# A decoder layer on one core: FFN matmuls with tokens on partitions, and the attention gate's columns moved to the beginning

## The chip, the cores and the metric

One Trainium2 chip, one NeuronCore of it. The metric is the device time of one execution in microseconds (us). TensorE (PE in the rows; PEld is its weight load), VectorE (DVE), ScalarE (ACT), GpSimd (POOL) and SyncE (SP, which starts nearly all DMAs) each run their own instruction stream in order and wait for one another on semaphores.

## The reference, cut to what matters

```python
h = rms_norm(x, norm_mix_pre)                       # x: 256 tokens x 1024
proj = h @ w_in                                     # 1024 x 9232
qa, ka, va, qd, kd, vd, zd, bd, ad, ga, gd = split(proj)   # 7 x 1024, then 8, 8, 1024, 1024
ya = attention(rope(qa), rope(ka), va)              # 8 heads x 128; one causal block of 256
yd = gated_deltanet(qd, kd, vd, zd, bd, ad, ...)    # conv, chunks of 64, a recurrence
merged = sigmoid(ga) * (ya @ w_o_attn) + sigmoid(gd) * (yd @ w_o_delta)
x = x + rms_norm(merged @ w_out, norm_mix_post)
h = rms_norm(x, norm_ffn_pre)
f = (silu(h @ w_gate) * (h @ w_up)) @ w_down        # 1024 -> 2816 -> 1024
x = x + rms_norm(f, norm_ffn_post)
```

## The kernel before, in words

Every weight comes from memory once, as a list `P` of pieces of about 512 KB. `load_to` issues their DMAs on SP into four buffers (`wr`); `split_to` cuts each piece into a high and a low part, ACT writing `wh` and DVE the remainder `wl`, and `piece(j)` asks for the split of piece j + 3. Each product of an activation and a weight is then three TensorE matmuls (high by high, high by low, low by high). There are two orientations. `natural` keeps the activation stationary and streams 512 weight columns, so tokens land on partitions: 12 matmuls of 512 columns for one piece. `chan` keeps the weight stationary and streams the 256 tokens, so channels land on partitions: 24 matmuls of 256 columns for one piece.

The program runs in this order. `start` loads x and its norm weights, transposes x through TensorE into `hT` (`x_transpose`, `x_evac`), and computes the first gate block ("g", 0): 414 columns, of which the first 16 are b and a and the rest belong to the attention gate. Then come the units of `make_units`: twelve "c" units (DeltaNet's q, k, v, in `chan` form), one attention or z unit after every second of them, then the last attention value unit ("a", 1, "v"), the last z unit ("z", 1), the gate blocks 1 and 2, the two halves of `w_o_attn` ("oa"), the gate blocks 3 and 4, and the two halves of `w_o_delta` ("od"). After that `main` does `w_out`, the FFN's gate and up products, and `w_down` (`two_tile`).

The recurrent and attention work (`dn_tile`, `dn_out`, `attn`) runs beside these as side generators. `Flow` keeps a planned time while the program is written, and `pump` writes a side step as soon as its inputs are planned to be ready; so the places of side steps between the main matmuls come out of that plan and are fixed in the program. The unit ("oa", 0) begins with `yield joined(("at", 0), ("at", 1))`: as long as both attention generators have not been written out, no main matmul is written. "od" waits in the same way for the DeltaNet outputs. `start` is written under `manual_schedule`, in its exact order.

In the FFN before, the first 512 channels of gate and up are done in token form: `silu` of the gate (scaled by `rs2`, one factor for each token) and the product with up, both per token tile, then eight 128x128 transposes back (`fn`, into `fT`). The other 2304 channels are done by `chan`, block by block: 24 matmuls for a gate block and 24 for an up block into one bank, a product with the row `rsb` that `spread` prepared, `silu`, a product, and a split into `fT`.

Of the kernel before, what the change touches and what calls it, by code (L numbers as in the profile page):

```python
# [18 lines left out]
D = 1024  # L19
# [6 lines left out]
NFB = DFF // 128  # L26
PSUM = bass.MemoryType.PSUM
# [37 lines left out]
def make_units():  # L65
    dn = [("c", g, p, hp) for g in range(2) for p in "qkv" for hp in range(2)]
    at = [("a", 0, p) for p in "qkv"] + [("z", 0)] + [("a", 1, p) for p in "qkv"] + [("z", 1)]
    at += [("g", n) for n in (1, 2)]
    out = [("g", 0)]
    i = 0  # L70
    for j, d in enumerate(dn):
        out.append(d)
        if j % 2 == 1:
            out.append(at[i])
            i += 1
    out += at[i:]
    out += [("oa", 0), ("oa", 1), ("g", 3), ("g", 4), ("od", 0), ("od", 1)]
    return out
# [173 lines left out]
def build(nc, tc, ctx, A):  # L252
# [79 lines left out]
    col0 = cst.tile([128, 8], F32, name="col0")  # L332
    triur = cst.tile([128, 128], F32R, name="triur")
# [35 lines left out]
    GB = []  # L369
    c = BA  # L370
    for i, n in enumerate((414, 414, 412, 412, 412)):
        GB.append((c, n))
        c += n
# [3 lines left out]
    for u in UNITS:  # L377
        if u[0] == "g":
            natblk(u, wind, *GB[u[1]])
# [15 lines left out]
    natblk(("fn", 0), A["w_gate"][0], 0)  # L395
    natblk(("fn", 1), A["w_up"][0], 0)
# [12 lines left out]
    def load_to(i):  # L409
        while nl[0] <= min(i, len(P) - 1):  # L410
# [3 lines left out]
            SP.dma_start(t, ap)  # L414
# [17 lines left out]
    def split_halves(j):  # L432
# [5 lines left out]
        for i in range(a):  # L438
            ACT.activation(hi[:, i], r[:, i], AF.Copy)
            DVE.tensor_tensor(lo[:, i], r[:, i], hi[:, i].bitcast(F32), op=ALU.subtract)  # L440
# [8 lines left out]

    xt = []  # L450
    for t in range(2):
        xx = s4.get([128, 1024], F32, f"x{t}")
        if t == 0:
            for q in range(2):
                SP.dma_start(xx[:, 512 * q:512 * q + 512], xd[0:128, 512 * q:512 * q + 512])
                if q == 0:
                    SP.dma_start(rows0, A["norm_mix_pre"].rearrange("o (k p) -> (o k) p", p=128))
            load_to(1)
        else:
            SP.dma_start(xx, xd[128:256, :])  # L460
        xt.append(xx)
    load_to(RAW - 1)
    SP.dma_start(rows[0:96], A["conv_w"][0].rearrange("i (b p) -> (i b) p", p=128))
# [37 lines left out]
    def x_evac(bs, cols, t, his, los, q):  # L501
# [6 lines left out]
        main_put(bs[1])  # L508

# [47 lines left out]
    def natural(j0, act, outs, first=0, end=4):  # L557
        his, los = act
        for i in range(first, end):
            hi, lo = piece(j0 + i)  # L560
            for kk in range(2):
# [419 lines left out]
    def gate_evac(i, outs):  # L981
        c0, n = GB[i]
        for st, base in ((sg, GA), (sd, GD)):
            lo, hi = max(c0, base), min(c0 + n, base + D)
            if hi <= lo:
                continue
            for t in range(2):
                if t not in st:
                    st[t] = yield from slot(s4, [128, 1024], F32, f"gt{base}{t}")
                ACT.activation(st[t][:, lo - base:hi - base], outs[t][:, lo - c0:hi - c0], AF.Sigmoid, scale=rs[t])  # L990
        for t in range(2):
            main_put(outs[t])
# [58 lines left out]
    def unit_g(u):  # L1051
        outs = yield from two_banks()
        yield from natural(plan[u], hT, outs)
        yield from gate_evac(u[1], outs)
# [43 lines left out]
    def start():  # L1098
        hT.extend((yield from act_slots("h")))
        with tc.manual_schedule():  # L1100
# [14 lines left out]
            ev = []  # L1115
            for q in range(2):
                ev.append((yield from x_transpose(xt[0], q)))
            fill(FILL)
            main_put(wb)
            outs = yield from two_banks()  # L1120
            x_evac(ev[0], col0, 0, hT[0], hT[1], 0)
            pc = [split_halves(0)]
            x_evac(ev[1], col0, 0, hT[0], hT[1], 1)
            pc.append(split_halves(1))

            def part(i, t):
                hi, lo = pc[i]
                n = hi.shape[2]
                ts = slice(128 * t, 128 * t + 128)
                for kk in range(2):  # L1130
                    k = 2 * i + kk
                    ah, al = hT[0][k // 4][:, k % 4, ts], hT[1][k // 4][:, k % 4, ts]
                    mm(outs[t][:, :n], ah, hi[:, kk, :], k == 0, False)
                    mm(outs[t][:, :n], al, hi[:, kk, :], False, False)
                    mm(outs[t][:, :n], ah, lo[:, kk, :], False, k == 7)

            part(0, 0)
            e0 = yield from x_transpose(xt[1], 0)
            part(1, 0)
            e1 = yield from x_transpose(xt[1], 1)  # L1140
            x_evac(e0, col0, 1, hT[0], hT[1], 0)
            pc.append(piece(2, 0))
            x_evac(e1, col0, 1, hT[0], hT[1], 1)
            part(0, 1)
            part(1, 1)
            nrs = {}
            for i in range(2):
                pc.append(piece(3, 0)) if i == 0 else None
                part(2 + i, 0)
                part(2 + i, 1)  # L1150
            for t in range(2):
# [6 lines left out]
                split_to(4 + t)  # L1158
            ACT.activation(ex, abc, AF.Exp)
            b = yield from main_bank()  # L1160
            tr(b[:, 0:105], rows[0:105, :], ident[0:105, 0:105])
            DVE.tensor_copy(colp[:, 0:105], b[:, 0:105])
            main_put(b)
            held.append(DVE.tensor_copy(id16, ident).ins)
        s4.put(xt[0], xt[1])
        for t in range(2):
            ACT.activation(beta[:, 8 * t:8 * t + 8], outs[t][:, 0:8], AF.Exp, scale=nrs[t])
# [193 lines left out]
```

## Time and profile before

| what | us |
|---|---|
| median of 3 runs | 551.74 |
| lowest and highest | 551.53, 552.23 |
| span of the profiled execution, first to last instruction | 550.8 |
| first gate matmul begins | 9.10 |
| first "c" matmul begins (the gate block of the beginning is done) | 21.12 |
| last z unit ends, gate block 1 begins | 233.99 |
| "od" begins | 308.54 |
| FFN blocks in `chan` form | 380.43 to 484.85 |
| last matmul begins | 544.7 |

The median is 0.98 us above the span, which begins at the first instruction and ends at the last. A row of the profile gives an engine, a line of the kernel (nearly all work passes through the helper lines 131, 289 and 293, so tiles tell more than lines), the operation, output and inputs, and the shape. For a matmul the input named first streams and the second is stationary. The busy time of a matmul row includes its drain, so successive rows overlap: what a matmul costs is the distance from its start to the next start.

### The profile page before, as it was taken

To read this page: it belongs to the slowest core of one execution; us is meant where nothing else is said; L and a number is where in the kernel's file an instruction comes from. 1 tells how busy PE (TensorE), PEld (TensorE's weight loads), DVE (VectorE), ACT (ScalarE), POOL (GpSimd) and SP (SyncE) were. 2 spreads that over 40 slices of the span, in tenths; PEclk is the share of its full clock that TensorE was granted. 3 is DMA by queue.
4 is the path that set the end of the run, shared out by engine and by line. 5 is a ranking of instruction groups with operands and counts; after the bars stand their busy time and mean duration, and the time that the engine had idled before them with its cause. 6 is when DMAs were issued, how large, how long until landed. Compare 5 with 4: busy or idle time off the path is not lost.

```text
span 550.8 us, 9219 instructions
## 1 busy us (share of the span) xinstructions
PE 538.2 (98%) x3554; PEld 480.8 (87%) x3554; DVE 383.4 (70%) x687; ACT 316.1 (57%) x569; POOL 26.5 (5%) x38
## 2 busy tenths in 40 slices
PE   7999999899999999999999999999999999999995
PEld 5988898898989888899889888778999999988884
DVE  4798886896879787866576566686666666754434
ACT  5968658588654966786526444584444444443331
POOL 0001002200000230000000000010000000000000
PEclk9999999999999999999999999999999999999999
DMA  7957765245465252245466765268666666655512
GB/s 243 240 154 226 227 192 153 78 116 157 126 178 155 79 166 63 62 147 156 128 202 192 246 221 175 74 175 252 186 191 186 175 181 187 192 190 190 193 39 76
DMA packets 89598, 90.45 MB, mean 164 GB/s; under 512 B 3169, under 2 KB 69842, under 8 KB 89554
## 3 DMA queue, kind: packets, MB, share of 16 engines
q1 hardware_dynamic: 89554, 89.86, 54.7%
q8 instruction: 28, 0.46, 0.4%
q14 instruction: 16, 0.13, 0.1%
HBM read 88.80 MB, written 1.05 MB: 163 GB/s over the span
## 4 chain that ended last, share of the span: by engine, by line
PE 85%; DVE 4%; ACT 3%; DMA 3%; issue 2%; POOL 2%; SPq 0%; POOLq 0%; DVEq 0%; ACTq 0%
PE b_m L289 74%; PE b_s L289 8%; PE b_s L293 2%; DMA q_x<-in_x 1%; DVE wl L131 1%; POOL tiny L131 1%; PE b_m L293 1%; DMA K<-in_shape_k 1%; DMA wr<-in_w_in 1%; ACT wh L131 1%; ACT L131 0%; DVE h_a L131 0%; DVE q_vT L131 0%; SPq L131 0%; ACT d_js L131 0%
## 5 line engine op out<-in xcount | busy, mean ns | idle before, releaser
L131 DVE TENSOR_TENSOR wl<-wr,wh 128x1024 fp32r<-128x1024 f32 (+3 forms) x168 | 197.9, 1184 | 91.5 <-ACT wh L131 87.5
L131 ACT ACTIVATE wh<-wr 128x1024 fp32r<-128x1024 f32 (+3 forms) x168 | 171.5, 1029 | 135.0 <-PE b_m L289 92.0
L289 PE MATMUL b_m<-wh,q_hh 128*128 128x512 f32 (+2 forms) x208 | 83.3, 400 | 1.3 <-ACT wh L131 1.3
L289 PE MATMUL b_m<-q_fh,wh 128*128 128x256 f32 x288 | 81.6, 283 | 0.0
L289 PE MATMUL b_m<-q_fl,wh 128*128 128x256 f32 x288 | 81.6, 283 | 0.0
L289 PE MATMUL b_m<-q_fh,wl 128*128 128x256 f32 x288 | 81.5, 283 | 0.0
L289 PE MATMUL b_m<-wl,q_hh 128*128 128x512 f32 (+2 forms) x208 | 78.9, 379 | 0.0
L289 PE MATMUL b_m<-wh,q_hl 128*128 128x512 f32 (+2 forms) x208 | 78.9, 379 | 0.0
L289 PE MATMUL b_m<-q_hh,wh 128*128 128x256 f32 x192 | 56.3, 293 | 0.0
L289 PEld LDWEIGHTS b_m<-q_fl,wh 128*128 128x128 f32 x288 | 55.3, 192 | 0.0
L289 PEld LDWEIGHTS b_m<-q_fh,wl 128*128 128x128 f32 x288 | 55.3, 192 | 0.0
L289 PEld LDWEIGHTS b_m<-q_fh,wh 128*128 128x128 f32 x288 | 55.3, 192 | 0.0
L289 PE MATMUL b_m<-q_hl,wh 128*128 128x256 f32 x192 | 54.4, 283 | 0.0
L289 PE MATMUL b_m<-q_hh,wl 128*128 128x256 f32 x192 | 54.3, 283 | 0.0
L289 PE MATMUL b_m<-wh,q_fh 128*128 128x512 f32 x120 | 46.9, 391 | 0.5 <-DVE q_fl L131 0.5
L289 PE MATMUL b_m<-wl,q_fh 128*128 128x512 f32 x120 | 46.9, 391 | 0.0
L289 PE MATMUL b_m<-wh,q_fl 128*128 128x512 f32 x120 | 46.6, 389 | 0.0
L289 PEld LDWEIGHTS b_m<-wh,q_hh 128*128 128x128 f32 x208 | 39.7, 191 | 6.1 <-ACT wh L131 2.2
L289 PEld LDWEIGHTS b_m<-wh,q_hl 128*128 128x128 f32 x208 | 39.6, 190 | 5.3
L289 PEld LDWEIGHTS b_m<-wl,q_hh 128*128 128x128 f32 x208 | 39.7, 191 | 3.9
L131 POOL TENSOR_TENSOR tiny<-tiny,mhalf 128x4 f32<-128x4 f32 (+1 forms) x20 | 17.4, 874 | 474.6 <-DVE tiny L131 474.6
L289 PEld LDWEIGHTS b_m<-q_hh,wh 128*128 128x128 f32 x192 | 36.7, 191 | 0.4
(215 smaller groups left out, 884.3 us busy)
## 6 DMA issues: line engine op xcount, KB each, us to landing
wr<-in_w_in SPq DMA_DIRECT2D x56, 512.0 KB, 4.1
wr<-in_w_gate SPq DMA_DIRECT2D x22, 512.0 KB, 3.9
wr<-in_w_up SPq DMA_DIRECT2D x22, 512.0 KB, 3.9
wr<-in_w_down SPq DMA_DIRECT2D x22, 512.0 KB, 3.3
wr<-in_w_in SPq DMA_DIRECT2D x12, 412.0 KB, 3.4
wr<-in_w_o_attn SPq DMA_DIRECT2D x8, 512.0 KB, 4.7
wr<-in_w_o_delta SPq DMA_DIRECT2D x8, 512.0 KB, 4.4
wr<-in_w_out SPq DMA_DIRECT2D x8, 512.0 KB, 3.6
```

The costliest lines, as they stand in the source:

```text
L131: r = f(*args, **kw)
L289: issue(lambda: PE.matmul(out, l, r, start=start, stop=stop))
L293: issue(lambda: PE.transpose(out, in_, idn))
```

## The change

1. FFN: all 2816 channels of gate and up are done in token form. Five rounds of 512 channels (`NFR`), each a `natural` pass over four gate pieces and four up pieces, then one pass whose pieces hold 256 gate columns beside 256 up columns. The result of each round is transposed back by `turn`, a generator that is put in `late` and is run after the first piece of the pass that follows. The `chan` blocks, `spread` of `rs2` and the tiles `js` are gone.
2. Beginning: `start` computes all 1024 columns of the attention gate for both token tiles, in eight pieces of 128 x 1024, into four banks, with the transposes of x put between them in pairs. x and the pieces are loaded whole, alternating; the norm weights come by a DMA of the ACT queue.
3. The 16 columns b and a are loaded apart (`wba`), cut into a high and a low part in a stationary tile of 128 columns (`wbr`), and multiplied with `hT` by 16 matmuls of 256 columns; two small matmuls with `sel` bring the result to tokens on partitions.
4. Units: the gate blocks 1 to 4 are gone from between the others. "g" is now the DeltaNet gate alone, two blocks of 512 columns, behind "oa". So ("z", 1) is followed at once by ("oa", 0).

```diff
@@ make_units
-    at += [("g", n) for n in (1, 2)]
-    out = [("g", 0)]
+    out = []
...
-    out += [("oa", 0), ("oa", 1), ("g", 3), ("g", 4), ("od", 0), ("od", 1)]
+    out += [("oa", 0), ("oa", 1), ("g", 0), ("g", 1), ("od", 0), ("od", 1)]
@@ plan
+    for k in range(8):
+        plan["ga", k] = len(P)
+        P.append((wind[k * 128:(k + 1) * 128, GA:GA + D].rearrange("(k p) n -> p k n", p=128), 1, D))
...
-    for b in range(4, NFB):
-        mark(("fg", b), chn, A["w_gate"][0], b * 128)
-        mark(("fu", b), chn, A["w_up"][0], b * 128)
+    for r in range(NFR):
+        natblk(("fg", r), wg, 512 * r)
+        natblk(("fu", r), wu, 512 * r)
@@ start
+            def part(pc, t, k):
+                hi, lo = pc
+                ts = slice(128 * t, 128 * t + 128)
+                ah, al = hT[0][k // 4][:, k % 4, ts], hT[1][k // 4][:, k % 4, ts]
+                for n in range(2):
+                    sl = slice(512 * n, 512 * n + 512)
+                    mm(outs[t][n], ah, hi[:, 0, sl], k == 0, False)
+                    mm(outs[t][n], al, hi[:, 0, sl], False, False)
+                    mm(outs[t][n], ah, lo[:, 0, sl], False, k == 7)
...
+            for k in range(8):
+                for i in range(2):
+                    mm(b[:, 0:256], wbr[:, k, :], hT[i][k // 4][:, k % 4, :], k == 0 and i == 0, k == 7 and i == 1)
...
+        for t in range(2):
+            mm(b[:, 16 * t:16 * t + 16], ba[:, 128 * t:128 * t + 128], sel, True, True)
@@ main, FFN
+        def turn(r, fn, nb):
+            yield from f_slots(r)
+            for t in range(2):
+                b = yield from main_bank()
+                for i in range(nb):
+                    tr(b[:, 128 * i:128 * i + 128], fn[t][:, 128 * i:128 * i + 128], ident)
+                ts = slice(128 * t, 128 * t + 128)
+                split_out(v4(b)[:, 0:nb], fT[r][0][:, 0:nb, ts], fT[r][1][:, 0:nb, ts])
...
-        yield from spread([rs2[0], rs2[1]], rsb)
+        late.append(turn(0, fn, 4))
+        for r in range(1, NFR):
+            fn = {}
+            for w in range(2):
+                outs = yield from two_banks()
+                yield from natural(plan["fu" if w else "fg", r], h2, outs, late=late)
```

How the instructions move is seen at three places. First the SP queue at the very beginning (`q0_x0`, `q1_x1` are the two token tiles of x, `wr0` to `wr3` the first pieces), before:

```order
L131 DMA q0_x0_98<-in_x 128x512
L131 DMA rows0_77<-in_norm_mix_pre 8x128
L131 DMA q0_x0_98<-in_x 128x512
L131 DMA wr0_102<-in_w_in 128x2x414
L131 DMA wr1_104<-in_w_in 128x2x414
L131 DMA q1_x1_106<-in_x 128x1024
L131 DMA wr2_108<-in_w_in 128x2x414
```

The same place in the changed kernel:

```order
L131 DMA q0_x0_100<-in_x 128x1024
L131 DMA wr0_102<-in_w_in 128x1024
L131 DMA q1_x1_104<-in_x 128x1024
L131 DMA wr1_106<-in_w_in 128x1024
L131 DMA wr2_108<-in_w_in 128x1024
L131 DMA wr3_110<-in_w_in 128x1024
L131 DMA wba_112<-in_w_in 128x8x16
```

The first weight piece is now second in the queue instead of fourth, and pieces are 512 KB instead of 414 KB.

Second the ACT engine around the end of the last z unit. `p0` and `p1` are the attention probabilities of head group 1 (the exponentials of the first and the second token tile), `sz01` and `sz11` the two halves of the z unit's `silu`, `ydh0` an output of DeltaNet group 0, `U` and `T` tiles of the triangular inverse of group 1. Before:

```order
L131 ACTIVATE d8_p0_2767,tiny_96<-b4_s_2769,tiny_96 128x128 x4
L131 ACTIVATE scr_97,tiny_96<-d1_oA_2356 128x128 x4
L131 ACTIVATE q15_p1_2768,tiny_96<-b1_s_2818,tiny_96 128x256 x2
L131 ACTIVATE q15_p1_2768,tiny_96<-b7_s_2835,tiny_96 128x256 x2
L131 ACTIVATE wh63_2910<-wr63_2594 128x828
L131 ACT_TABLE_LOAD
L131 ACTIVATE d13_sz01_2904<-b3_m_2588,tiny_96 128x512
L131 ACTIVATE q11_ydh0_2320<-b0_s_2876,colp_95 128x4x128
```

In the changed kernel:

```order
L131 ACTIVATE scr_98,tiny_97<-d1_oA_2461 128x128 x4
L131 ACTIVATE q16_p1_2843,tiny_97<-b4_s_2923,tiny_97 128x256 x2
L131 ACTIVATE wh67_3117<-wr67_2699 128x1024
L131 ACT_TABLE_LOAD
L131 ACTIVATE d13_sz01_2984<-b5_m_2693,tiny_97 128x512
L131 ACT_TABLE_LOAD
L131 ACTIVATE q16_p1_2843,tiny_97<-b1_s_2946,tiny_97 128x256 x2
L131 ACT_TABLE_LOAD
L131 ACTIVATE d7_sz11_2986<-b2_m_2694,tiny_97 128x512
L131 ACTIVATE q12_ydh0_2425<-b0_s_2988,colp_96 128x4x128
```

The second pair of p1 exponentials now stands behind `sz01`, the first half of z, and between two more table loads. On PE, 80 side matmuls (from the transposes of `d1_oA` and one level of the inverse, over the transposes of p0 and p1 and the products with v, to the last level) stand in one run between the last z matmul and the first "oa" matmul; before, they stand among 48 gate matmuls.

Third PE at the end of the FFN's first 512 channels (`d_fn` is the token-form product, `d_dg,ones` the matmul of `spread`), before:

```order
L289 MATMUL b_m<-wh_4156,q_fh_3839 128x512
L289 MATMUL b_m<-wl_4157,q_fh_3839 128x512
L289 MATMUL b_m<-wh_4156,q_fl_3840 128x512
L289 MATMUL b_m<-d_dg,ones 128x256
L293 MATMUL b_m<-ident,d_fn_4114 128x128 x4
L289 MATMUL b_m<-q_fh_3837,wh_4180 128x256
L289 MATMUL b_m<-q_fl_3838,wh_4180 128x256
L289 MATMUL b_m<-q_fh_3837,wl_4181 128x256
```

In the changed kernel, one piece later:

```order
L289 MATMUL b_m<-wh_4129,q_fh_3788 128x512
L289 MATMUL b_m<-wl_4130,q_fh_3788 128x512
L289 MATMUL b_m<-wh_4129,q_fl_3789 128x512
L293 MATMUL b_m<-ident,d_fn_4063 128x128 x4
L293 MATMUL b_m<-ident,d_fn_4090 128x128 x4
L289 MATMUL b_m<-wh_4170,q_fh_3788 128x512
L289 MATMUL b_m<-wl_4171,q_fh_3788 128x512
L289 MATMUL b_m<-wh_4170,q_fl_3789 128x512
```

The transposes stand 12 matmuls behind the last up matmul, and matmuls of 512 columns follow; such a place comes once in every round.

## Rows read from the trace of the kernel before

**Rows 1.** The page, part 1: busy us (share of the span) and instructions.

```profile
PE 538.2 (98%) x3554; PEld 480.8 (87%) x3554; DVE 383.4 (70%) x687; ACT 316.1 (57%) x569; POOL 26.5 (5%) x38
```

**Rows 2.** Timeline of PE (start us, us, instruction): FFN in `chan` form, then `w_down`.

```profile
384.05 0.28 PE L289 MATMUL b_m<-q_fh,wh 128*128 128x256 f32 x1
...
484.85 0.40 PE L289 MATMUL b_m<-wh,q_fh 128*128 128x512 f32 x1
...
533.84 0.39 PE L289 MATMUL b_m<-wh,q_fh 128*128 128x512 f32 x1
```

**Rows 3.** Timeline of PE: gate block 4, its last three pieces, to "od".

```profile
301.76 0.34 PE L289 MATMUL b_m<-wh,q_hh 128*128 128x412 f32 x1
...
308.54 0.39 PE L289 MATMUL b_m<-wh,q_ydh 128*128 128x512 f32 x1
```

**Rows 4.** Timeline of PE: eight transposes between 512-column matmuls, in "od".

```profile
321.24 1.09 PE L293 MATMUL b_m<-ident,q_gt 128*128 128x128 f32 x8
...
322.40 0.39 PE L289 MATMUL b_m<-wh,q_ydh 128*128 128x512 f32 x1
```

**Rows 5.** Timeline of PE: `spread` and the first four `fn` transposes in the FFN.

```profile
379.65 0.59 PE L289 MATMUL b_m<-d_dg,ones 128*128 128x256 f32 x2
...
380.43 0.36 PE L289 MATMUL b_m<-q_fh,wh 128*128 128x256 f32 x1
```

**Rows 6.** Timeline of all engines: the beginning (in brackets idle before, and what ended it).

```profile
5.44 1.11 PE L293 MATMUL b_m<-ident,q_x 128*128 128x128 f32 x4 [0.56 <-DMA q_x<-in_x]
...
6.34 1.49 PE L1110 MATMUL b_m<-warm 128*128 128x512 f16 x3
...
9.10 0.71 PE L289 MATMUL b_m<-wh,q_hh 128*128 128x414 f32 x1 [1.27 <-ACT wh L131]
...
9.61 0.55 PE L289 MATMUL b_m<-wh,q_hl 128*128 128x414 f32 x1
...
9.95 0.55 PE L289 MATMUL b_m<-wl,q_hh 128*128 128x414 f32 x1
...
21.12 0.36 PE L289 MATMUL b_m<-q_hh,wh 128*128 128x256 f32 x1
```

**Rows 7.** Windows: length, busy us (count) by engine, granted clock, DMA, GB/s; the end.

```profile
544.90:549.20 4.30, 0.00 (x0) 0.00 (x0) 2.17 (x4) 0.69 (x2) 0.55 (x1) 1.00 0.27 100
549.30:550.70 1.40, 0.00 (x0) 0.00 (x0) 0.00 (x0) 0.00 (x0) 0.00 (x0) 0.50 0.11 41
```

**Rows 8.** Timeline of ACT: around the end of the last z unit.

```profile
231.08 0.48 ACT L131 ACTIVATE q_p<-b_s,tiny 128x256 f32<-128x256 f32 x1 [0.29 <-DVE tiny L131]
...
232.90 1.28 ACT L131 ACT_TABLE_LOAD   x1
234.19 0.69 ACT L131 ACTIVATE d_sz<-b_m,tiny 128x512 f32<-128x512 f32 x1
234.78 0.69 ACT L131 ACTIVATE q_ydh<-b_s,colp 128x512 fp32r<-128x512 f32 x1
235.35 0.39 ACT L131 ACTIVATE h_U<-b_s 128x256 f16<-128x256 f32 x1
...
236.14 0.72 ACT L131 ACTIVATE d_sz<-b_m,tiny 128x512 f32<-128x512 f32 x1
...
238.54 1.13 ACT L131 ACTIVATE q_pT<-b_s 128x512 f32<-128x512 f32 x2
```

**Rows 9.** Timeline of PE: last z matmuls, products with v, gate block 2's first.

```profile
232.20 0.39 PE L289 MATMUL b_m<-wh,q_hl 128*128 128x512 f32 x1
...
233.99 0.35 PE L289 MATMUL b_m<-wh,q_hh 128*128 128x414 f32 x1
...
242.43 0.68 PE L289 MATMUL b_s<-q_pT,q_av 128*128 128x256 f32 x2
...
243.74 0.44 PE L289 MATMUL b_m<-wh,q_hh 128*128 128x414 f32 x1
...
248.61 0.35 PE L289 MATMUL b_m<-wh,q_hh 128*128 128x412 f32 x1
```

More of the change, by code (lines that the diff above doesn't have):

```diff
@@ L560, in natural @@
             hi, lo = piece(j0 + i)
+            if late and i == first + 1:
+                yield from late.popleft()
             for kk in range(2):
@@ L979, in two_banks, with gate_evac @@
         return [b0, b1]
[L981 to L990, printed above, removed]
+    def gate_evac(st, n, outs):
         for t in range(2):
+            if t not in st:
+                st[t] = yield from slot(s4, [128, 1024], F32, f"gt{t}")
+            ACT.activation(st[t][:, 512 * n:512 * n + 512], outs[t], AF.Sigmoid, scale=rs[t])
             main_put(outs[t])
@@ new lines, in start @@
+            part(pc[1], 1, 1)
+            xb[0, 6] = yield from x_tr(0, 6)
+            pc.append(piece(2, 0))
+            evac(0, 4)
+            part(pc[2], 0, 2)
+            part(pc[2], 1, 2)
+            xb[1, 4] = yield from x_tr(1, 4)
+            xb[1, 6] = yield from x_tr(1, 6)
+            pc.append(piece(3, 0))
+            evac(1, 4)
+            part(pc[3], 0, 3)
+            evac(0, 6)
+            part(pc[3], 1, 3)
+            evac(1, 6)
+            pc.append(piece(4, 0))
+            part(pc[4], 0, 4)
@@ L1146, in start @@
+            part(pc[4], 1, 4)
             nrs = {}
[L1147 to L1150, printed above, removed]
             for t in range(2):
@@ L1157, in start @@
                 DVE.tensor_scalar(nrs[t], rs[t], -1.0, None, op0=ALU.mult)
-                split_to(4 + t)
+                pc.append(piece(5 + t, 0))
+                part(pc[5 + t], 0, 5 + t)
+                part(pc[5 + t], 1, 5 + t)
+            wbr = yield from slot(s4, [128, 8, 128], F32R, "wbr")
+            DVE.memset(wbr.bitcast(F32), 0.0)
+            ACT.activation(wbr[:, :, 0:16], wba, AF.Copy)
+            DVE.tensor_tensor(wbr[:, :, 32:48], wba, wbr[:, :, 0:16].bitcast(F32), op=ALU.subtract)
+            DVE.tensor_tensor(sel, ident[0:48, 0:16], ident[0:48, 32:48], op=ALU.add)
             ACT.activation(ex, abc, AF.Exp)
+            pc.append(piece(7, 1))
+            part(pc[7], 0, 7)
+            part(pc[7], 1, 7)
             b = yield from main_bank()
@@ L1163, in start @@
             main_put(b)
+            b = yield from main_bank()
+            for k in range(8):
+                for i in range(2):
+                    mm(b[:, 0:256], wbr[:, k, :], hT[i][k // 4][:, k % 4, :], k == 0 and i == 0, k == 7 and i == 1)
+            s4.put(wbr)
+            ba = yield from slot(s1, [48, 256], F32, "ba")
+            ACT.activation(ba, b[0:48, 0:256], AF.Copy)
+            main_put(b)
             held.append(DVE.tensor_copy(id16, ident).ins)
@@ L1204, in two_tile @@
                 hi, lo = piece(plan[name, k])
+                if late and k == 1:
+                    yield from late.popleft()
                 for t in range(2):
@@ L1303, in main @@
-        for b_ in range(4, NFB):
-            if b_ % 4 == 0:
-                yield from f_slots(b_)
-            b = yield from main_bank()
-            yield from chan(plan["fg", b_], h2, b[:, 0:256])
-            yield from chan(plan["fu", b_], h2, b[:, 256:512])
-            js = yield from slot(s2, [128, 2, 256], F32, "js")
-            DVE.tensor_tensor(js, b.rearrange("p (a c) -> p a c", a=2), rsb[:, None, :].to_broadcast([128, 2, 256]),
-                              op=ALU.mult)
-            main_put(b)
-            ACT.activation(js[:, 0], js[:, 0], AF.Silu)
-            DVE.tensor_tensor(js[:, 1], js[:, 1], js[:, 0], op=ALU.mult)
-            split_out(js[:, 1], fT[-1][0][:, b_ % 4, :], fT[-1][1][:, b_ % 4, :])
-            s2.put(js)
+        late.append(turn(0, fn, 4))
@@ new lines, in main @@
+        for r in range(1, NFR):
[3 more added lines that the diff above has]
+                yield from natural(plan["fu" if w else "fg", r], h2, outs, late=late)
+                for t in range(2):
+                    if w == 0:
+                        yield from gate_out(fn, t, outs[t], 512)
+                    else:
+                        up_out(fn, t, outs[t])
+                    main_put(outs[t])
+            late.append(turn(r, fn, 4))
@@ L1322, in last @@
             yield 0
-        yield from two_tile("dn", ([a for a, _ in fT], [a for _, a in fT]), NFB, 4, finish_rms(wfo, x1, last))
+        yield from two_tile("dn", lambda k, ts: [a[:, k % 4, ts] for a in fT[k // 4]], NFB, 4, finish_rms(wfo, x1, last), late)
     def later(ns, gen):
```

152 lines of the change are left out of this document (86 added, 66 removed).

## The prediction

> **What bounds the kernel now.** I read the page's busy times first: TensorE is busy for 98% of the span, the next engine for 70% [rows 1]. So the first question for each edit is how much TensorE time it adds or takes, and the second is whether an edit makes TensorE wait where it does not wait now. For the first question busy means are of no use, because a matmul's row contains its drain; I took distances between starts from the timeline. In the FFN's `chan` form 840 matmuls of 256 columns lie between 384.05 and 484.85, which is 0.120 us each; in `w_down` 216 matmuls of 512 columns lie between 484.85 and 533.84, 0.227 each [rows 2]. The last 36 matmuls of 412 columns in the gate take 0.188 each [rows 3]. All three stretches run without a gap, so nothing but TensorE bounds them. For the second question I read the timelines of ACT and PE where the change takes main matmuls away from beside the side work.
>
> **The FFN.** 36 pieces change form. Each was 24 matmuls of 0.120, 2.88 us, and becomes 12 of 0.227, 2.72 us: 36 x 0.16 = 5.7 us less [rows 2]. In return all channels must be transposed back. Eight transposes in the middle of 512-column matmuls cost 0.93: from 321.24 to 322.40 there are 1.16 us, of which one matmul is 0.227 [rows 4]. Five rounds with eight and one with four make 5.1. Before, `spread` and the first four transposes cost 0.78 [rows 5] and the other four about half of 0.93; these 1.2 us go. The net is -5.7 + 5.1 - 1.2 = -1.8 us. A transpose could also wait for the product it turns: DVE has two passes over a 512-wide bank to do (about 0.7 each by the z evacuations on ACT, 0.69 [rows 8]), and TensorE has 12 matmuls, 2.7 us, to do meanwhile. I take that cover as enough; without it each of the six turns would lose up to about 0.5, so the bounds of this term are -2.2 and +1. The work on DVE and ACT falls (no `rsb` product, one `silu` over 512 columns in place of four over 256), but neither is the bound there, and I put it at nothing.
>
> Here a rule of the skill can be weighed. The Trainium skill (TensorE: Matmul & The Clock Gate, section Back-to-back issue gap) gives the gap of a matmul of N columns as N/2.4 + 2.5 ns, that is 109 ns for 256 and 216 ns for 512. By it the 36 pieces would save only about 1 us, and the FFN with its transposes would be slower, not faster. The rows show 120 and 227, and the sum goes by them.
>
> **The gate columns.** 240 matmuls of 412 or 414 columns at 0.188 are 45.1 us; 192 of 512 at 0.227 are 43.6: -1.5. The columns b and a now need 16 matmuls of 256 columns, 1.9 us at 0.120, and two small fp32 matmuls with `sel`. The trace has none of that shape; they are smaller than `spread`, which with four transposes took 0.78 [rows 5], so 0.1 to 0.6, and I take 0.4. Together +0.8.
>
> **The beginning.** Before, the first gate matmul starts at 9.10, after 1.27 us in which TensorE waited for the high part of the first piece; from there to the first "c" matmul at 21.12 it takes 12.0 us for 48 matmuls that at 0.188 are 9.0 [rows 3, 6]. About 1 us of the other 3 is the transposes of the second token tile, about 2 the lower clock: at 9.61 and 9.95 successive matmuls start 0.34 apart, not 0.188 [rows 6], which is the 1.2 GHz level. After the change the first piece is second in the queue instead of fourth, but x must be there whole before its first transposes, and the three warm matmuls (1.49 us from 6.34 [rows 6]) still stand ahead of the first gate matmul. If x lands when its second half lands now (5.44 [rows 6]), four transposes (1.1) and the warm ones bring the start to 8.0; if the larger transfers bring it a microsecond and a half sooner, 6.5. I take 7.5: -1.6, with 9.1 (nothing gained) and 6.2 as bounds. Four more transposes stand inside the stream, in four separate places: +0.8. The stretch at low clock costs about the same or, as TensorE hardly stops before the first piece, less: -0.3, bound -1.9. The chain of b and a, through an ACT copy behind four sigmoids, can hold TensorE a little before the "sel" matmuls: +0.3. The beginning comes to -0.8, bounds -4 and +1.5.
>
> **The place where the moved gate blocks were.** This term decides the sign. Before, gate block 1 begins at 233.99 and block 2 at 248.61 [rows 9]: 14.6 us, of which 48 gate matmuls at 0.188 are 9.0 and 5.6 are the side matmuls of attention group 1 and of the inverse. ACT works through its queue meanwhile, and nobody waits for it. After the change the gate matmuls are gone from here and "oa" may not be written before the attention is: those side matmuls stand in a row, and TensorE can only follow the chain on ACT. And that chain is longer than before, since ACT's own order changed: the second pair of exponentials stands behind `sz01`, which needs the last matmuls of z, and between two more table loads. I walk it by rows of now. The first z tile's last matmul ends about 232.6 [rows 9]. Then, start to start: `sz01` 0.59, load 1.28, two exponentials 0.9 (0.48 each, overlapping), load 1.28, `sz11` 0.59, `ydh0` 0.57, four U and T at 0.26, three copies of transposed probabilities at 0.57 [rows 8]: 8.0 us, so 240.7 with the latencies. Only then come the products with v: 242.43 to 243.74 is one group, 1.3 us [rows 9]; two groups and the small matmuls around them make 3.1. "oa" starts at 243.8. Had TensorE only the side matmuls to do, it would start at 233.99 + 5.6 = 239.6. The new wait is 4.2 us. Its lower bound leaves out the detour of the exponentials (both loads less, ACT's two weight splits gone): 2.4. Its upper bound lets the last level of the inverse, whose U and T stand behind the copies on ACT, come behind the products rather than beside them: 7.
>
> A second rule bears on this walk. The Trainium skill (ScalarE: Activation LUTs, section What ACT_TABLE_LOAD costs) puts a drain of about 1.38 us on top of each load. The two more loads would then lengthen the wait by an estimated 2.8 us. The trace shows a load from 232.90 of 1.28 us and the next activation at 234.19 [rows 8]: no drain, and none is in the sum.
>
> Behind it the DeltaNet chain of group 1 has 14 us less main work to hide beside. It still has about one 512-column piece for each step and ends one piece ahead of "od", so I add only 0.5, bounds -0.5 and +1.5.
>
> **Sum.** FFN -1.8, gate columns +0.8, beginning -0.8, new wait +4.2, chain +0.5: +2.9. The profiled span of 550.8 becomes 553.7; the median lies 0.98 above the span, so 551.74 becomes **554.6**.
>
> **The rivals.** (a) The lower clock in the new wait. The trace shows the granted clock still at 1.00 in the 4.3 us after the last matmul and at 0.50, 1.2 GHz, behind them [rows 7]; gaps now are shorter. In the new wait TensorE is idle for some 3 us and then has only transposes and small matmuls, so it may fall; "oa" would then begin as the gate did at 9.10, for about 2 us more: 556.6. (b) The wait is small: ACT has slack elsewhere, `sz01` is not late, the wait is at its lower bound 2.4, the chain behind costs nothing and the beginning gives 1.3 rather than 0.8: 551.7 - 1.8 + 0.8 - 1.3 + 2.4 = 551.8, no change. For it speaks that ACT is free for a good part of the span [rows 1]; against it, that its order is fixed and the exponentials cannot pass `sz01`. (c) Faster: the beginning. x and the first piece land early enough that the first gate matmul starts at 6.2, TensorE does not stop ahead of it and the low clock is over by then: -2.9 - 1.9 + 1.1 = -3.7, with the wait at 2.4 and nothing behind it: -2.3, 549.4. It decides from a start before about 6.8 with matmuls 0.227 apart from the first. (d) Each load stands ACT for as long again, as the rule on loads says: about 2.6 more by the load's own 1.28, 557.2. (e) The 256-column matmul is no dearer than half a 512-column one, as the rule on gaps nearly says, and the 5.7 us are not there: 560.3. The rows speak against (d) and (e).
>
> **How the numbers follow.** Forecast 0.48, (a) 0.13, (b) 0.20, (c) 0.15, (d) 0.02, (e) 0.02. A difference of 0.2%, 1.1 us, is about what a measurement of this kernel can tell from no change. The forecast's own range, from the bounds, is 552.3 to 557; (a), (d) and (e) lie on the slower side too, so slower has 0.65, the same 0.20, faster 0.15. A range from 550.6 to 557.8 leaves out most of (c), (e) and a tail of (a), no more than 2 in 10.
>
> **What would show it.** In the profile after: FFN pieces 2.72 us apart, with 0.9 us for eight transposes; a first gate matmul near 7.5 and a first "c" matmul near 35; on ACT three table loads around the z unit, and a TensorE idle of about 4 us in all between the last z and the first "oa" matmul, its longest piece released by DVE or ACT on `p`. The prediction is wrong if that idle is under 2 us, if the first gate matmul comes before 6.5, or if the transposes of the rounds wait.

## The result: 557.56 us, 1.0% slower

The changed kernel takes 557.56 us (median of 4 runs), the kernel before 551.73: a ratio of 1.0102 with a 95% interval of 1.0088 to 1.0115, some 5.8 us. Span against span it is 556.5 to 550.8, or 5.7, and the stages below are read from these two profiled executions: what a matmul costs is the distance from its start to the next start. The forecast was 554.6 (+2.9) with a range of 550.6 to 557.8.

| stretch, by its main matmuls | before | after | difference |
|---|---|---|---|
| start to the first "c" matmul, and the gate matmuls elsewhere | 21.12 + 37.35 | 37.21 + 22.56 | +1.3 |
| the 88 side matmuls between the last z matmul and "oa" (before: the same 88, among the last z matmuls and gate block 1) | 5.86 | 11.71 | +5.85 |
| FFN to the first `w_down` matmul, then `w_down` to the end of its matmuls | 128.55 + 60.02 | 125.90 + 60.48 | -2.2 |
| all else ("c" units +0.3, v and z +0.3, "oa" to "od" +0.4, `w_out` -0.3) | | | +0.7 |

Where two numbers stand in the first line, the second is the sum of the gate matmuls in the later blocks. (The order of PE told ahead of the prediction speaks of 80 side matmuls; the trace has 88. The last matmul of the kernel before begins at 544.49.) The busy times of the engines in the changed kernel, which answer to [rows 1]:

```profile
PE 539.7 (97%) x3128; PEld 456.3 (82%) x3128; DVE 369.9 (66%) x649; ACT 316.8 (57%) x549; POOL 26.7 (5%) x38
```

TensorE issues 426 matmuls fewer and is busy 1.5 us longer; its share falls from 98 to 97%. The span is 5.7 us longer, so the loss is mostly idle time, and the rows below show in which places.

The FFN in the changed kernel (timeline of PE: start, duration, instruction; in brackets idle before and its releaser), which answers to [rows 2] and [rows 5]:

```profile
364.13 0.50 PE L289 MATMUL b_m<-wh,q_fh 128*128 128x512 f32 x1 [0.54 <-DVE q_fl L131]
...
390.20 1.03 PE L293 MATMUL b_m<-ident,d_fn 128*128 128x128 f32 x8
391.00 0.47 PE L289 MATMUL b_m<-wh,q_fh 128*128 128x512 f32 x1
391.31 0.39 PE L289 MATMUL b_m<-wl,q_fh 128*128 128x512 f32 x1
...
490.03 0.39 PE L289 MATMUL b_m<-wh,q_fh 128*128 128x512 f32 x1
```

Eight transposes and the slower matmul behind them cost 1.11 (390.20 to 391.31) less one matmul of 0.227, that is 0.88, without a wait in front: no transpose waits for its product, in this round and in the five others.

The beginning, timeline of all engines:

```profile
6.92 0.79 PE L289 MATMUL b_m<-wh,q_hh 128*128 128x512 f32 x1
...
7.51 0.63 PE L289 MATMUL b_m<-wh,q_hl 128*128 128x512 f32 x1
...
7.94 0.63 PE L289 MATMUL b_m<-wl,q_hh 128*128 128x512 f32 x1
...
21.74 0.37 ACT L131 ACTIVATE q_hh<-b_m,col 128x128 fp32r<-128x128 f32 x1 [0.42 <-DVE q_hl L131]
22.01 1.05 ACT L131 ACTIVATE wh<-wr 128x1024 fp32r<-128x1024 f32 x1
...
23.11 0.50 PE L289 MATMUL b_m<-wh,q_hh 128*128 128x512 f32 x1 [1.28 <-ACT wh L131]
...
24.36 0.50 PE L289 MATMUL b_m<-wl,q_hh 128*128 128x512 f32 x1 [0.52 <-DVE tiny L131]
...
37.21 0.47 PE L289 MATMUL b_m<-q_hh,wh 128*128 128x256 f32 x1
```

The first gate matmul comes 2.2 us sooner than before (6.92 for 9.10 [rows 6]), at 0.43 from one to the next, which is the 1.2 GHz level (e7's rows at the end have this spacing with the granted clock at 0.50). At 23.11 TensorE waits 1.28 us for the high part of piece 4: its split begins only at 22.01, because six evacuations of transposed x stand ahead of it on ACT, behind the split of piece 3. The first waits 1.27 us for its transposes, and three others 0.42 us each for DVE. At 24.36 comes another 0.52, for the low part of piece 4 from DVE. Around these two waits eight steps of matmuls take 4.19 us (21.44 to 25.63) where they would take 1.8 at 0.228 each: 2.4 us are lost.

The place between z and "oa", ACT and PE, which answers to [rows 8] and [rows 9]:

```profile
248.74 1.28 ACT L131 ACT_TABLE_LOAD   x1
...
249.64 0.40 PE L289 MATMUL b_m<-wh,q_hl 128*128 128x512 f32 x1
...
250.04 0.69 ACT L131 ACTIVATE d_sz<-b_m,tiny 128x512 f32<-128x512 f32 x1
...
250.73 1.28 ACT L131 ACT_TABLE_LOAD   x1
252.03 0.47 ACT L131 ACTIVATE q_p<-b_s,tiny 128x256 f32<-128x256 f32 x1
...
253.06 1.28 ACT L131 ACT_TABLE_LOAD   x1
...
253.75 0.83 PE L293 MATMUL b_s<-ident,d_p 128*128 128x128 f32 x4 [2.81 <-DVE d_p L131]
...
257.78 1.20 PE L289 MATMUL b_s<-q_pT,q_av 128*128 128x256 f32 x2
...
261.58 0.48 PE L289 MATMUL b_m<-wh,q_yah 128*128 128x512 f32 x1
```

TensorE idles 2.81 us for the probabilities, and the chain on ACT is the one that was foretold: `sz01`, load, two exponentials, load. But `sz01` begins only when one more load, from 248.74, has ended. Windows of the same stretch (from:to, length, busy us and count of PE, PEld, DVE, ACT and POOL, granted clock, DMA share, GB/s) show the clock falling to 0.50, the 1.2 GHz level, after that idle, and rising again once the products with v run:

```profile
252.00:253.70 1.70, 0.00 (x0) 0.00 (x0) 0.59 (x3) 1.67 (x6) 0.00 (x0) 1.00 0.54 176
...
256.00:257.00 1.00, 0.86 (x12) 0.64 (x11) 0.93 (x3) 1.00 (x4) 0.00 (x0) 0.50 0.00 0
...
259.00:260.00 1.00, 1.00 (x15) 0.94 (x14) 0.00 (x0) 1.00 (x4) 0.00 (x0) 1.00 0.00 0
```

### The profile page after: what moved, and what is told of

Its sections match the earlier page's. It is cut to its first block, busy times and chain, and to the rows that moved or that the text cites. A ratio compares the mean times of both kernels' runs of the same rounds, so it can differ in the third digit from the quotient of the medians.

```text
span 556.5 us, 8301 instructions
## 1 busy us (share of the span) xinstructions
PE 539.7 (97%) x3128; PEld 456.3 (82%) x3128; DVE 369.9 (66%) x649; ACT 316.8 (57%) x549; POOL 26.7 (5%) x38
## 4 chain that ended last, share of the span: by engine, by line
PE 85%; ACT 5%; DVE 4%; issue 3%; POOL 2%; DMA 1%; POOLq 0%; DVEq 0%; ACTq 0%
PE b_m L289 73%; PE b_s L289 8%; PE b_s L293 2%; PE b_m L293 2%; POOL tiny L131 1%; DVE wl L131 1%; DMA wr<-in_w_in 1%; ACT wh L131 1%; DMA q_x<-in_x 1%; ACT L131 0%; POOL d_dc L131 0%; ACT q_hh L131 0%; ACT q_ga L131 0%; DVE h_a L131 0%; DVE q_vT L131 0%
## 5 line engine op out<-in xcount | busy, mean ns | idle before, releaser
L131 DVE TENSOR_TENSOR wl<-wr,wh 128x1024 fp32r<-128x1024 f32 (+1 forms) x164 | 197.6, 1209 | 117.1 <-ACT wh L131 116.7
L131 ACT ACTIVATE wh<-wr 128x1024 fp32r<-128x1024 f32 (+1 forms) x164 | 171.3, 1051 | 153.3 <-PE b_m L289 144.4
L289 PE MATMUL b_m<-wh,q_fh 128*128 128x512 f32 x264 | 103.6, 392 | 0.5 <-DVE q_fl L131 0.5
L289 PE MATMUL b_m<-wl,q_fh 128*128 128x512 f32 x264 | 102.9, 390 | 0.0
L289 PE MATMUL b_m<-wh,q_fl 128*128 128x512 f32 x264 | 102.7, 390 | 0.0
L289 PE MATMUL b_m<-wh,q_hh 128*128 128x512 f32 x192 | 79.8, 415 | 1.6 <-ACT wh L131 1.3
L289 PE MATMUL b_m<-wl,q_hh 128*128 128x512 f32 x192 | 76.2, 397 | 0.6 <-DVE tiny L131 0.5
L289 PE MATMUL b_m<-wh,q_hl 128*128 128x512 f32 x192 | 75.7, 394 | 0.0
L289 PEld LDWEIGHTS b_m<-wh,q_fh 128*128 128x128 f32 x264 | 49.6, 188 | 10.9 <-DVE q_fl L131 1.0
L289 PEld LDWEIGHTS b_m<-wl,q_fh 128*128 128x128 f32 x264 | 49.6, 188 | 10.7 <-DVE wl L131 0.7
```

Source lines behind the costliest of these rows:

```text
L131: r = f(*args, **kw)
L289: issue(lambda: PE.matmul(out, l, r, start=start, stop=stop))
```

## The experiments

Ratios are to the kernel before, with 95% intervals; the changed kernel stands at 1.0102.

**e1: the FFN alone.** The kernel before with part 1 of the change (the plan of the pieces, `turn`, `late`, `gate_out` and `up_out` as in the diff above) and nothing else.

> The kernel before with part 1 of the change alone (FFN all in token form); beginning and order of the units as before. Theory (the loss is all in the beginning and at the join of z and oa; the FFN gains what its pieces say): in the trace of after the FFN and w_down with the end are 2.2 us shorter than before (128.55 to 125.90 for the FFN, w_down 0.5 longer), so 551.7 - 2.2 = 549.5 us, and the join and the beginning look as before. Rival (the token form of the FFN brings nothing by itself, for instance because its transposes wait when the stage is entered at another moment): 551.7 or more.

Measured: 549.46 us, ratio 0.9961 (0.9946 to 0.9975). Timeline of PE, first FFN matmul and first `w_down` matmul:

```profile
356.65 0.50 PE L290 MATMUL b_m<-wh,q_fh 128*128 128x512 f32 x1 [0.56 <-DVE q_fl L132]
...
482.46 0.39 PE L290 MATMUL b_m<-wh,q_fh 128*128 128x512 f32 x1
```

125.8 us where the kernel before has 128.55. So part 1 is a gain of some 2.2 us, and the rest of the change loses about 8.

**e2, e3: gate blocks back between z and "oa".**

```diff
-    out += [("oa", 0), ("oa", 1), ("g", 0), ("g", 1), ("od", 0), ("od", 1)]
+    out += [("g", 0), ("g", 1), ("oa", 0), ("oa", 1), ("od", 0), ("od", 1)]   # e2
+    out += [("g", 0), ("oa", 0), ("oa", 1), ("g", 1), ("od", 0), ("od", 1)]   # e3
```

> The changed kernel with the two DeltaNet gate blocks put between the last z unit and oa, where gate blocks 1 and 2 stood before; nothing else is changed. Theory (main matmuls are missing beside the side work at the join): of the 11.7 us between the last z matmul and the first oa matmul some 5.9 are side matmuls at their full-clock price of before, the other 5.8 are waiting and lower clock; with 21.8 us of gate matmuls there TensorE does not wait, the granted clock stays at 1.00 and most of the 5.8 comes back: 557.6 - 5.3 = 552.3, range 551.7 to 553. Rival (the chains of attention and DeltaNet need that time in any order, and the wait only moves to the place ahead of od): 557 to 558, with a wait of 4 us or more ahead of od.

> The changed kernel with one of the two DeltaNet gate blocks between the last z unit and oa, the other left behind oa. Run e2 with both blocks there gave 554.7, with the side work of DeltaNet reaching into od and TensorE held up there. Theory (each half of the side work needs main matmuls beside it: the join some 6 us, the DeltaNet steps the rest): one block of 10.9 us is enough for the join, the DeltaNet steps end further ahead of od, and the total is 553.5, range 553.0 to 554.3, below e2. Rival (DeltaNet's steps take about 50 us from the last level of the inverse on, however the blocks stand, and the inverse ends later with each block put ahead of oa): no better than e2, 554.7 to 555.7.

Measured: e2 554.70, ratio 1.0053 (1.0037 to 1.0068); e3 554.33, ratio 1.0043 (1.0029 to 1.0056). In e2 TensorE no longer waits at the join, and half of the 5.8 us is back, not nearly all. All side matmuls from the first "c" matmul to the FFN, summed from start to start, take 62.2 us in e2, as in the kernel before (62.4), where the changed kernel has 68.4. But 2.7 of these 6.2 us turn up again on main matmuls: the 96 of "od" take 23.5 us instead of 21.9, those of "oa" 23.2 instead of 22.9, the gate blocks 23.3 instead of 22.6.

e3's median lies between the ranges of its two texts (554.3 and less, 554.7 and more), and by the intervals it is no better than e2. Its profiled execution had a beginning 1.4 us longer than e2's, with a fall of the granted clock to 0.50 (read from 24.8 to 27.4) that e2's did not have; from the first "c" matmul to the FFN e3 takes 322.7 us and e2 323.4. So one gate block may be a little better than two, and these runs do not settle it.

What lies on the main matmuls of "od" is the DeltaNet chain. Its length can be read from two matmuls, the first of the last level of the inverse (`wl,h_T`) and the last transposes of its output (`d_oA`). Timeline of PE, kernel before:

```profile
246.59 0.41 PE L289 MATMUL b_s<-wl,h_T 128*128 128x64 f16 x8
...
300.17 0.60 PE L293 MATMUL b_s<-ident,d_oA 128*128 128x128 f32 x4
```

Changed kernel:

```profile
261.35 0.40 PE L289 MATMUL b_s<-wl,h_T 128*128 128x64 f16 x8
...
312.42 0.95 PE L293 MATMUL b_s<-ident,d_oA 128*128 128x128 f32 x4
...
316.66 0.39 PE L289 MATMUL b_m<-wh,q_ydh 128*128 128x512 f32 x1
```

e2:

```profile
270.75 0.29 PE L289 MATMUL b_s<-wl,h_T 128*128 128x64 f16 x4
...
322.31 0.44 PE L293 MATMUL b_m<-ident,q_gt 128*128 128x128 f32 x2 [0.40 <-DVE q_gt L131]
322.59 0.32 PE L293 MATMUL b_s<-ident,d_oA 128*128 128x128 f32 x1
```

e3:

```profile
268.06 0.28 PE L289 MATMUL b_s<-wl,h_T 128*128 128x64 f16 x4
...
319.27 0.59 PE L293 MATMUL b_s<-ident,d_oA 128*128 128x128 f32 x2 [1.02 <-DVE d_oA L131]
```

53.6 us in the kernel before, then 51.1, 51.8 and 51.2, whatever main matmuls lie beside it. Gate blocks ahead of "oa" cover the join, but they put the end of the inverse later (261.35, 268.06, 270.75), and the chain then reaches into "od", where its steps hold TensorE up by a few tenths each, and by 1.02 us at once in e3. The mechanism of the rival in e3's text holds, though its range does not. The places of these steps come out of the plan, so the runs do not tell a length that the chain has in any plan; that TensorE waits for `d_oA` and `q_gt` in e2 and e3 shows that the plan has them no later than they are ready. In the kernel before the chain ends 8.4 us ahead of "od" at 308.54 [rows 3]; in the changed kernel the main work that was moved to the beginning is missing behind it, and only 4.2 us are left.

**e4: fill the wait.** Eleven f16 matmuls into a free bank, just ahead of the transposes of p0 (`warms[0]` is the zero tile of the warm matmuls).

```diff
+        if g == 1:
+            fb = psp.tile([128, 512], F32, name="fill", tag="b5")
+            for _ in range(11):
+                issue(lambda: PE.matmul(fb, warms[0][:, 0:128], warms[0], start=True, stop=True))
```

> The changed kernel with 11 more f16 matmuls of 512 columns on TensorE, into a bank that is free then, behind the last transposes and small matmuls ahead of the wait for the probabilities p; their result is not read. Every other instruction keeps its place on every engine. In the trace of after TensorE is idle there from 250.9 to 253.75, and the granted clock is at 0.50 (1.2 GHz) from about 255 to 258.6. Theory (the lower clock is a cost of its own, caused by TensorE's standing idle, and half of those 3.6 us is lost): the fill ends before p is ready, the clock stays at 1.00 through the stretch, oa begins 1.6 us sooner, total 556.0. Rival (in that stretch TensorE follows ACT's chain anyway, so its clock costs nothing): clock at 1.00, but oa begins at the same time, total 557.6. Second rival (the clock falls in spite of the fill): 557.6 with 0.50 in the rows.

Measured: 557.48, ratio 1.0100 (1.0085 to 1.0115). Timeline of PE, and one window as above:

```profile
249.16 0.40 PE L289 MATMUL b_m<-wh,q_hl 128*128 128x512 f32 x1
...
253.33 0.82 PE L293 MATMUL b_s<-ident,d_p 128*128 128x128 f32 x4 [0.46 <-DVE d_p L131]
...
260.66 0.48 PE L289 MATMUL b_m<-wh,q_yah 128*128 128x512 f32 x1
```

```profile
256.00:257.00 1.00, 0.80 (x17) 0.61 (x17) 0.74 (x2) 1.00 (x4) 0.00 (x0) 1.00 0.00 0
```

The clock stays at 1.00, so the idle stretch was what let it fall. But from the last z matmul to "oa" it is 11.5 us instead of 11.9: the fall costs 0.4, not 1.6, and the total shows nothing. TensorE follows ACT there, and a slower TensorE mostly fills its own waits. The first rival holds nearly whole.

**e7: the exponentials ahead of z.** The `silu` of the last z unit is written behind the p1 exponentials on ACT.

```diff
+        exps.extend([er.ins] * g)                    # the last exponential of group 1
...
-            ACT.activation(z, v4(outs[t]), AF.Silu, scale=rs[t])
+                if n == 1:
+                    with tc.issue_after(exps[0]):
+                        ACT.activation(z, v4(outs[t]), AF.Silu, scale=rs[t])
...
+            fl.add("silus", silus())                 # as a side generator
```

> The changed kernel with one thing moved on ACT: the two halves of silu(z) of the last z unit stand behind the second pair of p1 exponentials; two of the three table loads there fall away with it. All other engines keep their order. Theory (the wait at the join is ACT's chain to the probabilities, lengthened by sz01 and two loads): the last exponentials are done at about 251.0 instead of 252.8, the transposes of p0 begin at 251.9 instead of 253.75, the copies of pT0 at 255.1 instead of 256.6, oa begins 1.5 us sooner or a little more, the granted clock does not fall or falls for less time; total 557.6 - 1.7 = 555.9. Rival (the wait is set by something else, DVE's divisions or the last levels of the inverse): oa begins within 0.4 us of 261.6, total 557.2 to 557.8.

Measured: 556.27, ratio 1.0077 (1.0055 to 1.0099). Timeline of PE:

```profile
250.58 0.40 PE L289 MATMUL b_m<-wh,q_hl 128*128 128x512 f32 x1
...
252.79 0.83 PE L293 MATMUL b_s<-ident,d_p 128*128 128x128 f32 x4 [0.91 <-DVE d_p L131]
...
260.68 0.47 PE L289 MATMUL b_m<-wh,q_yah 128*128 128x512 f32 x1
```

10.1 us instead of 11.9 from the last z matmul to "oa": 1.8 for the detour, as expected. (e7's times here lie 0.9 later: its beginning took 1.8 us longer in this execution, and half of it came back before the join. The last section returns to that. The four executions lie at 554.99, 555.43, 557.10 and 557.27 us; the profiled one is the slowest.) About 4 of the 5.85 us remain. TensorE stands idle for 1.9 of them, in four pieces, of which 0.91 is for the probabilities; the rest isn't told apart here.

**e5, e5b: the order in the beginning.** e5 puts the splits of pieces 4 to 6 ahead of the last evacuations and of the squares; e5b also moves the zeroing of `wbr` to the start of DVE's queue, and its copy and the squares behind the split of piece 7.

```diff
             evac(1, 4)
             part(pc[3], 0, 3)
-            evac(0, 6)
+            pc.append(piece(4, 0))
             part(pc[3], 1, 3)
-            evac(1, 6)
-            pc.append(piece(4, 0))
+            evac(0, 6)
+            pc.append(piece(5, 0))
...
             DVE.memset(ones, 1.0)
+            wbr = yield from slot(s4, [128, 8, 128], F32R, "wbr")
+            DVE.memset(wbr.bitcast(F32), 0.0)        # e5b: first on DVE
...
+            pc.append(piece(7, 1))                   # e5b: ahead of the squares and of wbr's copy
             ACT.activation(wbr[:, :, 0:16], wba, AF.Copy)
```

> The changed kernel with three places of its hand-written beginning exchanged: the splits of pieces 4, 5 and 6 stand ahead of the last two pairs of transposed columns and of the two squares of x on ACT and DVE; the matmuls keep their order. Theory (the gate block of the beginning is held up by ACT's order, 1.28 us ahead of piece 4 and 0.5 us and 0.25 us inside it): those waits go, nothing of the data lands later than it is needed (the piece loads land by about 16 to 22.5 us), first c matmul at 35.3 instead of 37.2, total 555.7. Rival (the loads set the pace there, or the sigmoids and the squares come due later and hold the first c matmuls instead): first c matmul within 0.5 us of 37.2 and total 557.1 to 557.6.

> Run e5 with three more places exchanged in the beginning: the zeroing of wbr stands at the very start of DVE's queue, its copy and the two squares of x behind the split of the last gate piece. In e5 the early splits took 2.0 us out of pieces 3 to 5, and 2.8 us came back at pieces 6 and 7, where the split of piece 7 stood on ACT behind a 2.25 us wait for that zeroing. Theory (the beginning is held up by the order on ACT and DVE alone): now nothing waits, first c matmul at 35.0 to 35.5, total 555.4. Rival (TensorE has to wait for the norm's square root on the GpSimd engine and the sigmoids at the end of the block in any order): first c matmul not before 36.5, total 557 or more.

Measured: e5 558.66, ratio 1.0117 (1.0099 to 1.0135), no gain. e5, timeline of all engines:

```profile
30.05 0.91 DVE L131 MEMSET q_wbr<- 128x1024 f32 x1 [0.16 <-issue]
...
30.99 0.31 ACT L131 ACTIVATE q_wbr<-wba 128x128 fp32r<-128x128 f32 x1 [2.25 <-DVE q_wbr L131]
...
32.40 0.50 PE L289 MATMUL b_m<-wh,q_hh 128*128 128x512 f32 x1 [0.61 <-ACT wh L131]
```

The waits at piece 4 went, and a new one took their place at piece 7: ACT stands 2.25 us for the zeroing of `wbr` on DVE, which stands behind the norm's square roots on POOL. (The split of piece 7 follows the copy of `wbr` at 31.31.) e5b takes that away too, and then it holds: 555.16, ratio 1.0055 (1.0040 to 1.0071), first "c" matmul at 34.64:

```profile
34.64 0.47 PE L289 MATMUL b_m<-q_hh,wh 128*128 128x256 f32 x1
```

**e10: both repairs, e5b and e2.**

> The changed kernel with the repairs of e5b (order in the beginning) and e2 (both gate blocks between the last z unit and oa) together. Theory (two separate losses that add): ratio to the kernel before 1.0102 - 0.0047 - 0.0049 = 1.0006, total 552.3; what is left of the 8.1 us that the beginning and the order of the units cost beside the FFN's gain is 0.8 of gate columns and about 2 of TensorE held up at the DeltaNet steps, which end inside od. Rival (the DeltaNet chain of some 51 us from the last level of the inverse on sets the end of od, and starts no earlier relative to the rest): the two do not add, 553.5 or more.

Measured: 551.70, ratio 0.9988 (0.9979 to 0.9998). The two add, and a little more; with e1's 0.9961 as the best that part 1 alone gives, some 1.5 us of the 8 are left. They lie where they lie in e2: "od" takes 23.5 us here, 1.6 more than before, "oa" 0.35 more. The beginning and the gate matmuls together are even (35.28 + 23.31 against 21.12 + 37.35).

**e8, e9: the loads' order for the kernel before.** e8 is e1 with the first loads as in the changed kernel; e9 also takes two copies of constants out of the beginning.

```diff
+    ACT.dma_start(rows0, A["norm_mix_pre"].rearrange("o (k p) -> (o k) p", p=128))
+        SP.dma_start(xx, xd[128 * t:128 * t + 128, :])
+        load_to(t)
...
-        ACT.activation(triur, triu, AF.Copy)
-        DVE.tensor_copy(mask16, maskT1)
+        with tc.issue_after(held[1]):                # e9: behind the beginning
+            ACT.activation(triur, triu, AF.Copy)
+        with tc.issue_after(held[0]):
+            DVE.tensor_copy(mask16, maskT1)
```

> Run e1 (the kernel before with the FFN in token form, 549.5 us) with the order of the first loads of the changed kernel: x whole, the first weight piece second in the queue, the norm weights on the ACT queue; nothing else. Theory (the changed kernel's first gate matmul at 6.9 instead of 9.1 comes from the order of the loads, not from the wider pieces): first gate matmul at about 7.0, and the two microseconds are kept: total 547.6, range 547.0 to 548.3. Rival (the second token tile and the next pieces are then late, and the first part of the gate waits for them): first gate matmul at 7 but first c matmul within 0.5 us of 21.2, total 549.2 to 549.8.

> Run e8 (before's program with the FFN in token form and the loads of the changed kernel's order) with the two copies of constants out of K, triur on ACT and mask16 on DVE, moved behind the beginning. In e8 the first gate matmul came at 7.03 but ACT and DVE then stood 2.0 and 2.2 us for K's transfer with those copies at the head of their queues, and TensorE waited 1.23 us at 13.9 for hT behind them. Theory (the order on ACT and DVE, not the loads, eats the earlier start): the wait goes, first c matmul at 19.4 or earlier instead of 20.6, ratio to the kernel before 0.9945 (e8 0.9969), total near 548.8. Rival (the next late thing, a gate piece or a side step, takes its place): ratio 0.996 to 0.998.

Measured: e8 550.27, ratio 0.9969 (0.9957 to 0.9981), no better than e1. e9 547.65, ratio 0.9914 (0.9899 to 0.9929), the fastest kernel of this study. e8, DVE and PE:

```profile
13.36 0.23 DVE L132 CAST mask<-K 128x128 f16<-128x128 f32 x1 [2.18 <-DMA K<-in_shape_k]
```

```profile
7.03 0.80 PE L290 MATMUL b_m<-wh,q_hh 128*128 128x414 f32 x1
...
13.90 0.45 PE L290 MATMUL b_m<-wh,q_hl 128*128 128x414 f32 x1 [1.23 <-DVE q_hl L132]
...
18.58 0.46 PE L290 MATMUL b_m<-wl,q_hh 128*128 128x414 f32 x1 [0.24 <-DVE wl L132]
...
20.59 0.36 PE L290 MATMUL b_m<-q_hh,wh 128*128 128x256 f32 x1
```

e9, PE:

```profile
6.91 0.72 PE L290 MATMUL b_m<-wh,q_hh 128*128 128x414 f32 x1
...
9.50 0.45 PE L290 MATMUL b_m<-wh,q_hh 128*128 128x414 f32 x1 [0.49 <-ACT wh L132]
...
18.21 0.36 PE L290 MATMUL b_m<-q_hh,wh 128*128 128x256 f32 x1
```

In e8 the work starts 2 us sooner than in the kernel before and then meets a copy that is written behind the beginning (in `gates`) and that the scheduler has put in the middle of it: DVE stands 2.18 us for the transfer of K with the parts of `hT` behind it, and TensorE 1.23. Moving the copies ends that, and gives more than its text expected (0.9914 for 0.9945). Of the 2.4 us between 20.59 and 18.21, 1.5 are this wait with the slower start behind it, and 0.5 a second one, at 18.58, that is gone too. The first gate piece gives little: its matmuls stand 0.19 apart instead of 0.34, but TensorE then waits 0.49 for the next split.

## Why the prediction had the right sign and half the size

The measured 557.56 lies 0.2 us inside the stated range, and 0.6 outside the one that the forecast's own bounds gave (552.3 to 557). The wider range took in rivals (a) and (d), of which (a) gave 0.4 us and (d) nothing; that it held is luck.

**The FFN** (forecast -1.8, measured -2.2; e1 alone the same). Piece by piece as worked out: 2.72 for 2.88, turns of 0.88, no waits. The small miss is two terms: `spread` and the transposes that go cost 1.5, not 1.2, and the turns 4.9, not 5.1. Rival (e) falls: the Trainium skill's gap for an isolated matmul (TensorE: Matmul & The Clock Gate, section Back-to-back issue gap) gives 109 ns for 256 columns and 216 for 512 where the rows have 120 and 227, and by it the FFN would have become slower; e1 is faster.

**The gate columns and the beginning** (forecast 0.0, measured +1.3). The start was right, 6.92 for 7.5. The step that failed is the term for waits behind it: the walk priced transposes and the clock, and of the waits only 0.3 us at the "sel" matmuls (0.30 in the trace). It never followed the split of piece 4 through ACT's new queue. The evacuations of transposed x stand ahead of it, and the waits of 1.28 and 0.52 us cost 2.4 with the slower starts around them. e5b shows the cause: its first "c" matmul comes 2.6 us sooner, and the term would be -1.3. e5 shows that there was a second cause behind the first.

**The place where the gate blocks were** (forecast +4.2, measured +5.85). The mechanism was right, and so was the chain: from `sz01` to the first products with v it is 7.7 us by rows (250.04 to 257.78) where the walk had 8.1 (232.6 to 240.7). The mis-sized step is the anchor. The walk let `sz01` begin at the end of the first z tile's matmuls, 232.6, which is 1.4 us ahead of the end of z. But in the kernel before `sz01` begins at 234.19, behind a table load from 232.90 [rows 8], 0.2 us after the end of z, and the walk left this load out. It is the same in the changed kernel: load from 248.74, `sz01` at 250.04, 0.2 us after the end of z at 249.87. So the products come 7.9 us after the end of z instead of 6.7: +1.2. The tail from there to "oa" is 3.8 instead of 3.1, of which e4 gives 0.4 to the lower clock; and the side matmuls that TensorE has to do anyway take 5.86, not 5.6, which brings the wait down by 0.26. So rival (a) happened, at a fifth of its price: TensorE's clock fell to the 1.2 GHz level as it said, but where TensorE only follows ACT that is nearly free. Rival (d) falls: a load from 250.73 takes 1.28 us and the next activation starts at 252.03, and again at 253.06 and 254.36, so the drain that the Trainium skill puts behind each load (ScalarE: Activation LUTs, section What ACT_TABLE_LOAD costs) isn't in these rows. e7 gives the two loads' detour 1.8 us, which is the distance that the prediction put between its value and its lower bound.

**The DeltaNet chain and the rest** (forecast +0.5, measured +0.7). The size was near, but the reason given, "one piece ahead of od", hid what matters: this chain took 51 to 54 us in all four orders of the units, so what stands before the end of the inverse and what stands behind it can't be traded freely. e2 and e3 show it.

Summed: -2.2 + 1.3 + 5.85 + 0.7 = 5.65, against 5.7 between the spans. Of the 2.8 that were missing, 1.65 come from the anchor and tail of the join, 1.3 from the beginning and 0.2 from the rest, and the FFN takes 0.4 off. Rivals (b) and (c) needed a join at its lower bound 2.4; e7, which takes the detour away but leaves ACT's weight splits, still has about 4. What stays open is why the first gate piece runs at the lower clock in some kernels and not in others; there is one profiled execution of each.

## What to carry to other kernels

Main matmuls beside a chain of small steps are its cover: before moving them, follow the chain on the other engines from the instruction that really starts it, in the new order. In a hand-ordered beginning, look at each weight split and ask what stands ahead of it on ACT and DVE; after taking one wait away, look again, since the next may eat the gain (e5, e8). And time the parts of a change one by one: here a gain of 0.4% lay under a loss of 1.4%.

## What the runs showed of the hardware

The granted clock fell to 0.50 (1.2 GHz) behind an idle of 2.81 us and light work after it, and stayed at 1.00 where that idle was filled; yet the total didn't move.

In e7 the two waits at piece 4 (1.29 and 0.53 us) were followed by matmuls 0.43 apart, as these rows of PE show, with the granted clock at 0.50 from 25.6 to 28.6, the 1.2 GHz level; so it was in e3 (1.32 and 0.53). In the profiles of the changed kernel, e2 and e4 the same waits (1.28 to 1.33 and 0.52 to 0.53) were followed by matmuls 0.23 apart. The waits there therefore cost 2.4 us in one execution and 4.0 in another.

```profile
25.61 0.63 PE L289 MATMUL b_m<-wh,q_hh 128*128 128x512 f32 x1
...
26.04 0.63 PE L289 MATMUL b_m<-wh,q_hl 128*128 128x512 f32 x1
```
